# Lambda's powers prepared in the fourth instead of the third block of the first projection, with the background queue of the fourth block pumped from its step 15 on at a rate of 0.9

## The chip, the cores and the metric

The kernel runs on one core of a Trainium2 chip. The metric is the device time of one execution in microseconds (us). Before the change three runs gave 1845.58, 1846.15 and 1850.67 us; the median is 1846.15.

## What is computed

Two layers on a sequence of 256 frames of width 2048, in float32. Each layer modulates its input by a conditioning vector c, runs a token mixer of inner width 4096, and closes with a gated residual and a LayerNorm. The first mixer is gated linear attention (GLA), the second a complex diagonal state-space layer (S5).

```python
mod = jnp.einsum('bd,lde->lbe', jax.nn.silu(c), ada_w) + ada_b[:, None, :]
for i in range(DEPTH):
    shift, scale, gate = jnp.split(mod[i], 3, axis=-1)
    u = x * (1.0 + scale[:, None, :]) + shift[:, None, :]
    h = gla_mixer(u, ...) if i % N_MIXERS == 0 else s5_mixer(u, ...)
    x = layer_norm(DEEPNORM_ALPHA * x + (1.0 + gate[:, None, :]) * h, ln_g[i], ln_b[i])
```

In the GLA mixer `proj = u @ w_in` gives q, k, v, z and a low-rank gate. In the S5 mixer each of 256 groups of 16 channels has 64 complex states. Their eigenvalues lambda come from small tables, and what the change touches is this:

```python
dt = jnp.exp(log_dt.astype(f32))[:, None]
mag = jnp.exp(a_re * dt)
lb_re = mag * jnp.cos(a_im * dt)
lb_im = mag * jnp.sin(a_im * dt)
```

The kernel needs the powers lambda^1 to lambda^8 and a coefficient that scales the S5 input matrix B.

## The kernel before

Everything is issued by one Python program for one core; a scheduler then fixes the order of instructions on each engine by the program's order and by its own estimate of when an instruction's inputs and buffers are ready. So an instruction can be issued somewhat ahead of its place in the program, but each engine's queue is fixed when the kernel is built.

Matrix products run in a split form: `wload` brings a weight tile of 128x1024 (512 KB, two 128-row groups by 512 columns) by a DMA of SyncE's queue, and `split` (lines 145, 146) makes a high part `hi` by a copy on ScalarE (ACT) and a low part `lo` by a subtraction on VectorE (DVE). Six weight tiles and three `hi` and three `lo` buffers rotate. One step consumes one weight tile. A step for v (`mv_step`) is 12 matmuls of 512 columns, one for q and k (`st_step`, called q below) is 24 of 256 columns.

The first projection computes q, k and v of the first layer. It is cut into four blocks along the contraction, `blocks = ((0, 2), (2, 2), (4, 4), (8, 8))` in units of 128, so that it can start before all of the modulation is known. Each later block adds to what the block before has left in `vtok` and `qk`. The first two blocks have 12 steps each, the third has 24 (16 for v, then 8 for q), the fourth has 48 (16 for q, then 32 for v). The steps are counted through all blocks as j, and within a block as i. While a block runs, the modulation for the next one is made: loads of `ada_w` (tiles `a`, 1 MB, 8 KB per partition), matmuls `psa` from them, the columns `mods`, transposes of x (`psx`) and the split of u. These are set to steps by a table (`put_ada`, `put_u`, list `along`) and may not be issued before that step. The last of them, the u of the fourth block, stand at steps j = 42 to 47.

One pool, `s8`, of twelve buffers of 8 KB per partition holds very different tiles: four for u, two for q and k (`qk`), two for x (`xrow`, until the third block's end), the modulation loads `a`, and all the tiles of the S5 preparation.

Work that nothing in the projection needs is put between the steps in three ways:
- `prep_lambda` (lines 500 to 596) is a generator. `next(lam, None)` runs it up to its next `yield`. It loads three tables, yields three times, computes dt and the magnitude by a polynomial in many small DVE instructions, two Sin on ACT, the powers by doubling (1, 2, 4 at a time, into `pwr`, with `pwt` for products), and ends with 64 small matmuls for `l8`. It takes 13 calls, and holds three buffers of 8 KB: `lamst`, `pwr` and `pwt`. Before, it gets a call in each step of the third block; what is left would run at that block's end.
- `bg` is the background queue. `pump(rate)` adds the rate to a counter and issues an item for each whole unit. Its first 26 items are the S5 preparation: loads, `prep_pow(0)` and `prep_pow(1)` (ACT copies `pd`, PE transposes `pspw`, ACT copies `lc`, a write of `rec`), `prep_b` (six DVE products `bb`, then four times transposes `psrb` and a copy `rowsb`, a write) and `prep_c` (`cc`, `psrc`, `rowsc`). `prep_pow` and `prep_b` need lambda's powers. Behind them come 108 items of the modulation of later stages. Before, the fourth block pumps from its first step at 0.62.
- `gla_gate` is a generator for the GLA gate. It gets a call in each step of the fourth block from i = 20 (`GATE_AT`) on and takes 17. It asks for the two 8 KB tiles `ea` and `la` with its third call. Its result multiplies k, and then `qs` is made from q (three DVE instructions, line 832). The attention matmuls `psst` start right behind the fourth block and need `qs`.

Then come the z projection with the attention output, the output projection, and the S5 layer. The S5 layer reads `rec` and `l8`. All later stages pump the same queue `bg`.

Of the kernel before, what the change touches and what calls it, by code (L numbers as in the profile page):

```python
# [33 lines left out]
def trunk(ctx, tc, x, c, ln_g, ln_b, ada_w, ada_b, gla_w_in, gla_gate_w2, gla_gate_b, gla_norm_g,  # L34
# [61 lines left out]
    def pump(rate=1.0):  # L96
        pace[0] += rate
        while pace[0] >= 1.0:
            pace[0] -= 1.0
            if bg:  # L100
                bg.pop(0)()
# [276 lines left out]
    def issue_to(n):  # L378
        while len(issued) < min(n, len(wants)):
            issued.append(wload(win, *wants[len(issued)]))  # L380
# [89 lines left out]
    def prep_small():  # L470
        dr = rp.tile([P, 2, 16], F32, tag="row", name="dr", bufs=2)
        dma(dr, s5_d[0].rearrange("(h g i) -> g h i", h=2, i=16))
        ps = psx("psd")
        for h in range(2):
            PE.transpose(ps[:16, h * P:(h + 1) * P], dr[:, h, :], ident)
        S.copy(dT, ps[:16, 0:256])
        zt = rp.tile([P, 448], F32, tag="row", name="zt", bufs=2)
        V.memset(zt, 0.0)
        for i in range(2):
            wdma(dk[:, i * 448:(i + 1) * 448].rearrange("(r p) c -> p r c", p=P), zt.unsqueeze(1).to_broadcast([P, 4, 448]))  # L480
# [195 lines left out]
    lam = prep_lambda()  # L676
# [5 lines left out]
    for part in range(2):  # L682
        for j in range(4):
            bg.extend(ada_dve(1, part, j))
    V_RATE, Z_RATE, OP_RATE = 0.62, 0.944, 0.755
    KEEP = (4, 6)
    GATE_AT = 20
    SCAN_RATE = 1.728
# [114 lines left out]
    for n, steps in enumerate(all_steps):  # L803
        for i, f_ in enumerate(steps):
            if n < 3:

                issue_to(j + 6)
            f_()
            with tc.issue_after(last_lo[0]), tc.issue_after(last_mm[0]):
                for g_ in along.get(j, ()):  # L810
                    g_()
            j += 1
            if n == 2:
                next(lam, None)
            elif n == 3:
                if i == 3:
                    prep_small()
                pump(V_RATE)
                if i >= GATE_AT:
                    next(gate, None)  # L820
        if n == 2:
            for _ in lam:
                pass

    for _ in gate:
        pass
# [83 lines left out]
    for g in range(8):  # L910
# [9 lines left out]
        for f in range(4):  # L920
            i = (g * 4 + f) % 8
# [271 lines left out]
    for g in range(8):  # L1193
        banks = [psm(f"su{g}{f}") for f in range(4)]
        for kp in range(8):
# [12 lines left out]
            n = max(0, int(b_pace[0]))  # L1208
# [67 lines left out]
    for g in range(8):  # L1276
# [9 lines left out]
        for f in range(4):  # L1286
            i = (g * 4 + f) % 8
# [43 lines left out]
    for g in range(8):  # L1331
# [14 lines left out]
        for f in range(4):  # L1346
            i = g * 4 + f
# [112 lines left out]
```

## Time and profile before

| | |
|---|---|
| median of three runs | 1846.15 us |
| the profiled execution | 1846.54 us, its span 1844.7 us |
| PE busy | 1795.5 us, 97% of the span |
| DVE busy | 1422.5 us, 77% |
| ACT busy | 897.4 us, 49% |
| third block, v part | 105.5 to 170.0 us |
| third block, q part | 170.0 to 203.3 us |
| fourth block, q part | 203.3 to 257.7 us |
| fourth block, v part | 257.7 to 362.8 us |

PE is TensorE's matmul, DVE is VectorE, ACT is ScalarE, SP is SyncE, whose queue issues the loads. Times inside the trace count from the span's start. An engine's busy time is the union of its instructions; in a list of groups each instruction counts fully, so where neighbours overlap, as they do by some 0.09 us on DVE and ACT, the groups add up to a little more. A wait is idle time of the engine just before an instruction, put down to the instruction whose end released it.

### The profile page before, as it was taken

How to read it: one execution, taken by the hardware profiler on the slowest of the kernel's cores; microseconds unless marked ns; L12 is line 12 of the kernel's file. 1: busy time of each engine (PE TensorE's matmuls, PEld its weight loads, DVE VectorE, ACT ScalarE, POOL GpSimd, SP SyncE). 2: the span in 40 equal slices, each digit the busy share in tenths (PEclk: the TensorE clock that was granted, in tenths of full speed). 3: DMA queues.
4: the chain of work that ended last, by engine and by line, in shares of the span. 5: the costliest groups of instructions: out<-in, count | busy, mean ns of one | idle time of the engine just before them, and what ended most of it. 6: DMA issues, size and time to landing. Idle time of an engine off the chain costs nothing.

```text
span 1844.7 us, 33886 instructions
## 1 busy us (share of the span) xinstructions
PE 1795.5 (97%) x13619; PEld 1588.5 (86%) x13619; DVE 1422.5 (77%) x1890; ACT 897.4 (49%) x1252; POOL 72.7 (4%) x78
## 2 busy tenths in 40 slices
PE   7999999999999999999999999999999999999997
PEld 5776897899999888899999999988888888888885
DVE  4877657879989888697899689888677775557556
ACT  5433557556556333654454454545544444444332
POOL 0000000000000000002223200000000000000000
PEclk9999999999999999999999999999999999999999
DMA  9996875889889998465654477899688886668653
GB/s 343 386 333 248 294 244 164 279 261 325 291 286 317 333 353 281 163 220 158 183 151 147 139 214 222 235 246 238 224 276 264 276 271 206 191 189 325 194 184 92
DMA packets 243798, 449.48 MB, mean 244 GB/s; under 512 B 19572, under 2 KB 48942, under 8 KB 242358
## 3 DMA queue, kind: packets, MB, share of 16 engines
q1 hardware_dynamic: 239320, 436.02, 73.9%
q0 software_dynamic: 3552, 10.24, 1.8%
q8 instruction: 107, 1.75, 0.4%
q10 hardware_dynamic: 768, 1.05, 0.2%
q14 instruction: 51, 0.42, 0.1%
HBM read 432.81 MB, written 14.42 MB: 242 GB/s over the span
## 4 chain that ended last, share of the span: by engine, by line
PE 86%; DVE 8%; DMA 3%; ACT 2%; issue 2%; SPq 0%; DVEq 0%; ACTq 0%
PE gl L192 13%; PE gl L193 7%; PE op L168 6%; PE op L167 6%; PE op L169 6%; PE z L182 3%; PE z L180 3%; PE z L181 3%; PE sz L180 3%; PE v L168 3%; PE v L169 3%; PE sz L181 3%; PE sz L182 3%; PE v L167 3%; PE su L180 2%; PE su L182 2%
## 5 line engine op out<-in xcount | busy, mean ns | idle before, releaser
L146 DVE TENSOR_TENSOR logl<-wgl,higl 128x1024 fp32r<-128x1024 f32 x128 | 156.5, 1224 | 115.3 <-ACT higl L145 113.7
L145 ACT CAST higl<-wgl 128x1024 fp32r<-128x1024 f32 x128 | 134.4, 1051 | 172.2 <-PE gl L192 167.9
L192 PE MATMUL gl<-yb,higl 128*128 128x512 f32 x512 | 179.6, 395 | 0.0
L192 PE MATMUL gl<-yp,higl 128*128 128x512 f32 x512 | 179.3, 395 | 0.1
L145 ACT CAST hio<-wo 128x1024 fp32r<-128x1024 f32 x95 | 100.2, 1055 | 155.3 <-PE op L169 127.3
L146 DVE TENSOR_TENSOR loo<-wo,hio 128x1024 fp32r<-128x1024 f32 x95 | 116.2, 1225 | 67.2 <-ACT hio L145 63.7
L315 DVE SCALAR_TENSOR_TENSOR acc<-wa,cs,acc 128x512 f32<-128x512 f32 x217 | 162.2, 748 | 4.8 <-DMA wa<-in_ada_w 2.1
L180 PE MATMUL su<-u1h,hisu 128*128 128x256 f32 x512 | 153.5, 301 | 1.9 <-DVE vv L1108 1.9
L180 PE MATMUL sz<-u1h,hisz 128*128 128x256 f32 x512 | 149.7, 292 | 1.2 <-ACT zs L1290 1.2
L180 PE MATMUL z<-u0h,hiz 128*128 128x256 f32 x512 | 148.7, 290 | 0.0
L182 PE MATMUL su<-u1h,losu 128*128 128x256 f32 x512 | 145.7, 286 | 0.4 <-DVE losu L146 0.4
L181 PE MATMUL su<-u1l,hisu 128*128 128x256 f32 x512 | 145.8, 285 | 0.0
L182 PE MATMUL z<-u0h,loz 128*128 128x256 f32 x512 | 144.9, 283 | 0.6 <-DVE loz L146 0.6
L182 PE MATMUL sz<-u1h,losz 128*128 128x256 f32 x512 | 144.9, 283 | 0.0
L181 PE MATMUL sz<-u1l,hisz 128*128 128x256 f32 x512 | 144.7, 283 | 0.0
L181 PE MATMUL z<-u0l,hiz 128*128 128x256 f32 x512 | 144.7, 283 | 0.0
L193 PE MATMUL gl<-yb,logl 128*128 128x256 f32 x512 | 143.4, 280 | 0.0
L193 PE MATMUL gl<-yp,logl 128*128 128x256 f32 x512 | 142.0, 280 | 0.0
L145 ACT CAST hisz<-wsz 128x1024 fp32r<-128x1024 f32 x64 | 66.9, 1051 | 107.2 <-PE sz L181 55.1
L192 PEld LDWEIGHTS gl<-yb,higl 128*128 128x128 f32 x512 | 96.0, 188 | 22.6
L192 PEld LDWEIGHTS gl<-yp,higl 128*128 128x128 f32 x512 | 95.8, 188 | 22.6 <-issue 0.6
L145 ACT CAST hisu<-wsu 128x1024 fp32r<-128x1024 f32 x64 | 66.7, 1050 | 95.1 <-PE su L181 70.6
(322 smaller groups left out, 5019.8 us busy)
## 6 DMA issues: line engine op xcount, KB each, us to landing
wgl<-in_s_w_glu SPq DMA_DIRECT2D x128, 512.0 KB, 4.7
wa<-in_ada_w SPq DMA_DIRECT2D x116, 512.0 KB, 5.1
wv<-in_gla_w_in SPq DMA_DIRECT2D x64, 512.0 KB, 6.1
wz<-in_gla_w_in SPq DMA_DIRECT2D x64, 512.0 KB, 5.2
wsu<-in_s_w_in SPq DMA_DIRECT2D x64, 512.0 KB, 3.7
wsz<-in_s_w_in SPq DMA_DIRECT2D x64, 512.0 KB, 4.3
wo<-in_s_w_out SPq DMA_DIRECT2D x64, 512.0 KB, 4.5
a<-in_ada_w SPq DMA_DIRECT2D x31, 1024.0 KB, 10.7
```

Of the source, the lines that this page charges most:

```text
L145: S.copy(hi, w)
L146: last_lo[0] = V.tensor_tensor(lo, w, hi.bitcast(F32), op=ALU.subtract).ins
L167: PE.matmul(banks[tt], lhsT=uh, rhs=hi[:, kk, :], start=(k == first), stop=False)
L168: PE.matmul(banks[tt], lhsT=uh, rhs=lo[:, kk, :], start=False, stop=False)
L169: last_mm[0] = PE.matmul(banks[tt], lhsT=ul, rhs=hi[:, kk, :], start=False, stop=(k == last)).ins
L180: PE.matmul(o, lhsT=wh, rhs=u.hi(k), start=(k == first), stop=False)
L181: PE.matmul(o, lhsT=wh, rhs=u.lo(k), start=False, stop=False)
L182: last_mm[0] = PE.matmul(o, lhsT=wl, rhs=u.hi(k), start=False, stop=(k == last)).ins
L192: PE.matmul(banks[f], lhsT=hi[:, kk, fs], rhs=u.both(k), start=(k == 0), stop=False)
L193: PE.matmul(banks[f][:, :T], lhsT=lo[:, kk, fs], rhs=u.hi(k), start=False, stop=(k == last))
L315: V.scalar_tensor_tensor(acc[0], w[:, kk, :], cs[:, k:k + 1], acc[0], op0=ALU.mult, op1=ALU.add)
```

## The change

The call of `next(lam, None)` goes from the third block (n == 2) to the first 15 steps of the fourth (n == 3), and what remained of it behind the third block goes. In those 15 steps the background queue isn't pumped; from step 15 on it is, at 0.9 items per step where it was 0.62 in all 48 steps. `gla_gate` and `prep_small` stay at their steps.

```diff
-    V_RATE, Z_RATE, OP_RATE = 0.62, 0.944, 0.755
+    V_RATE, Z_RATE, OP_RATE = 0.9, 0.944, 0.755
+    LAM_TO = 15
...
-            if n == 2:
-                next(lam, None)
-            elif n == 3:
+            if n == 3:
                 if i == 3:
                     prep_small()
-                pump(V_RATE)
+                if i < LAM_TO:
+                    next(lam, None)
+                else:
+                    pump(V_RATE)
                 if i >= GATE_AT:
                     next(gate, None)
-        if n == 2:
-            for _ in lam:
-                pass
```

## Rows read from the trace of the kernel before

**Rows 1.** The page: busy time, share of the span and instructions of each engine; and the shares of the chain that ended last, by engine.

```profile
PE 1795.5 (97%) x13619; PEld 1588.5 (86%) x13619; DVE 1422.5 (77%) x1890; ACT 897.4 (49%) x1252; POOL 72.7 (4%) x78
...
PE 86%; DVE 8%; DMA 3%; ACT 2%; issue 2%; SPq 0%; DVEq 0%; ACTq 0%
```

**Rows 2.** Busy time by stretch: start and end, length, then busy us and (instructions) of PE, PEld, DVE, ACT, POOL, the granted clock, the DMA share, GB/s. The stretches are the v and the q part of the third block, the q and the v part of the fourth.

```profile
105.50:170.00 64.50, 59.02 (x358) 40.35 (x357) 51.78 (x125) 19.72 (x27) 0.00 (x0) 1.00 0.75 262
170.00:203.30 33.30, 33.30 (x277) 28.34 (x275) 21.16 (x37) 11.99 (x16) 0.00 (x0) 1.00 0.92 331
203.30:257.70 54.40, 52.53 (x437) 51.62 (x436) 35.16 (x47) 34.96 (x40) 5.00 (x5) 1.00 0.83 269
257.70:362.80 105.10, 102.87 (x482) 82.49 (x480) 79.64 (x95) 62.09 (x67) 3.65 (x4) 1.00 0.70 217
```

**Rows 3.** What PE waited for from 105 to 204 us, the third block: total us, times, longest.

```profile
PE v L168 <- DVE lov L146: 3.8, 2, 1.9
PE v L167 <- ACT hiv L145: 1.6, 1, 1.6
```

**Rows 4.** The same from 204 to 363 us, the fourth block.

```profile
PE v L168 <- DVE lov L146: 1.8, 3, 0.7
PE pspw L610 <- ACT pd L603: 1.0, 1, 1.0
PE pspw L610 <- ACT lc L612: 0.8, 2, 0.4
PE psrb L624 <- DVE bb L652: 0.5, 1, 0.5
```

**Rows 5.** What SyncE's queue waited for before modulation loads (L254) from 105 to 205 us: the release of an older load by its matmuls, and the release of `lamst`.

```profile
SPq L254 <- PE psa L275: 29.4, 6, 9.3
SPq L254 <- DVE crci L510: 9.7, 1, 9.7
```

**Rows 6.** DVE's timeline in the third block's v part, from the first writing of `pwr`: start, length, instruction.

```profile
152.37 0.49 DVE L510 TENSOR_TENSOR pwr<-lamst 128x128 f32<-128x128 f32 x2
...
155.54 1.22 DVE L146 TENSOR_TENSOR lov<-wv,hiv 128x1024 fp32r<-128x1024 f32 x1
...
160.49 1.22 DVE L146 TENSOR_TENSOR lov<-wv,hiv 128x1024 fp32r<-128x1024 f32 x1
```

**Rows 7.** Busy time of the third block's v part again, DVE's part (and, in the first row, ACT's) of the instructions that touch `lamst` alone, and of those that touch `pwt` alone.

```profile
105.50:170.00 64.50, 11.27 (x47) 0.51 (x2) 1.00 0.75 262
105.50:170.00 64.50, 8.04 (x18) 1.00 0.75 262
```

**Rows 8.** DVE's timeline: the first of `prep_b(0)`'s six products.

```profile
224.14 1.22 DVE L647 TENSOR_TENSOR bb<-bin,crci 128x1024 f32<-128x1024 f32 x1
```

**Rows 9.** ACT's groups by line from 204 to 258 us, the fourth block's q part: busy us, mean ns of one, idle before them.

```profile
L612 ACT ACTIVATE lc<-pspw,kst 128x512 f32<-128x512 f32 x4 | 4.4, 1208 | 0.0
L625 ACT COPY rowsb<-psrb 128x512 f32<-128x512 f32 x4 | 4.3, 1086 | 0.0
L612 ACT ACTIVATE lc<-pspw 128x512 f32<-128x512 f32 x4 | 4.1, 1138 | 0.0
L603 ACT COPY pd<-pwr 128x1024 f32<-128x1024 f32 x4 | 4.0, 1045 | 0.0
...
L669 ACT COPY cc<-cin 128x1024 f32<-128x1024 f32 x1 | 1.1, 1081 | 0.0
```

**Rows 10.** PE's groups by line: the transposes of `prep_pow` and `prep_b` in the fourth block's q part, and the matmuls for `l8` in the third block's v part.

```profile
L610 PE MATMUL pspw<-ident,pd 128*128 128x128 f32 x32 | 4.5, 280 | 1.9 <-ACT pd L603 1.0 <-ACT lc L612 0.8
L624 PE MATMUL psrb<-ident,bb 128*128 128x128 f32 x16 | 2.5, 278 | 0.0
...
L591 PE MATMUL psl<-ident,pwr 128*32 128x32 f32 x64 | 1.0, 199 | 0.0
```

**Rows 11.** PE's timeline: two neighbouring matmuls of a v step in the third block, and two of a q step in the fourth.

```profile
129.04 0.39 PE L167 MATMUL v<-hiv,u0h 128*128 128x512 f32 x1
129.27 0.39 PE L168 MATMUL v<-lov,u0h 128*128 128x512 f32 x1
...
218.08 0.28 PE L180 MATMUL q<-u0h,hiq 128*128 128x256 f32 x1
218.20 0.28 PE L181 MATMUL q<-u0l,hiq 128*128 128x256 f32 x1
```

**Rows 12.** Busy time by stretch, columns as in rows 2: the middle of the fourth block's v part.

```profile
290.00:326.00 36.00, 33.77 (x152) 26.24 (x151) 33.47 (x44) 30.81 (x34) 2.23 (x2) 1.00 0.55 164
```

**Rows 13.** ACT's groups by line from 258 to 363 us, the fourth block's v part: Exp (L726) and Ln (L729) of the gate with their table loads.

```profile
L726 ACT ACT_TABLE_LOAD x2 | 2.6, 1283 | 0.0
L729 ACT ACT_TABLE_LOAD x2 | 2.6, 1283 | 0.0
L729 ACT ACTIVATE ea<-ea,ones 128x1024 f32<-128x1024 f32 x2 | 2.3, 1152 | 0.0
...
L726 ACT ACTIVATE ea<-ea 128x1024 f32<-128x1024 f32 x2 | 2.1, 1062 | 0.0
```

**Rows 14.** The instructions that touch `qs` up to 365 us: count, shortest, median and longest in ns, then the first and last start.

```profile
L846 PE MATMUL psst<-qs,qk x20: 272/352/430, 362.8 to 364.8; 128*64 128x256 f32 x8, 128*64 128x192 f32 x8, 128*64 128x128 f32 x4
L832 DVE TENSOR_TENSOR qs<-qk,ft x3: 1219/1751/2285, 333.3 to 343.2; 128x2048 f32<-128x2048 f32 x1, 128x1536 f32<-128x1536 f32 x1, 128x1024 f32<-128x1024 f32 x1
```

**Rows 15.** SyncE's queue in order of time: lambda's first load.

```profile
101.94 0.46 SPq L513 DMA_DIRECT2D lamst<-in_s_a_re  x1
```

## The prediction

> **What bounds the kernel now.** I read the page's busy shares and its chain first: PE is busy for 97% of the span and holds 86% of the chain that ended last [rows 1]. So an edit pays only where PE stands idle, and costs only where it makes PE idle. Next I cut the time around the change into four stretches (the third block's v part, its q part, the fourth block's q part, its v part) and compared PE busy with each length [rows 2]: PE is idle for 5.5, 0.0, 1.9 and 2.2 us. That is all there is to win here. The PE waits name it. In the third block two waits for a weight split (`lov`) come to 3.8 us, one for `hiv` to 1.6 us [rows 3]; in the fourth, three waits for `lov` come to 1.8 us, `prep_pow` (`pspw`) to 1.8 us, `bb` to 0.5 us [rows 4]. No wait there is for a modulation load, though SyncE's queue stood 29.4 and 9.7 us before such loads for a buffer to come free [rows 5].
>
> **The change, part by part.** PE's work is the same; it is moved. So the sum is one of PE waits, against the profiled execution's own 1846.54 us (span 1844.7, so 1.8 us lie around it); the median of the runs is 0.4 us lower.
>
> *Third block.* The two `lov` waits are lambda's: in the DVE timeline a string of small instructions on `lamst`, `pwr` and `pwt` stands before the split that starts at 155.54 and, with evictions of v, before that at 160.49, the two for which PE waited [rows 6]. Without them DVE loses about 20 us of work: 11.3 us on `lamst`, 8.0 us on `pwt`, and some small ones [rows 7], so 51.8 of 64.5 us becomes about 32. Nothing is late next: ACT is busy for 19.7 us there [rows 2]. Term: -3.8 us (between -3.8 and -2, if some other DVE work is late in a wait's place). The 1.6 us wait for `hiv` at the block's start stays; lambda's arithmetic has not begun there. Three buffers come free for the modulation loads, and SyncE's queue loses lambda's three loads in this block; as PE waited for no such load, and was busy for all 33.3 us of the q part, I cost this at nothing. What hides it is the six weight tiles fetched ahead.
>
> *Fourth block, q part (16 steps).* Leaves: the background queue. `prep_b(0)`'s six products of 1.22 us go from DVE [rows 8]; from ACT go two `prep_pow`, 12.5 us (4.4 + 4.1 + 4.0), four `rowsb` copies, 4.3 us, and `cc`, 2.2 us [rows 9]. Comes: lambda, 13 pieces at steps 0 to 12; the first three only load and wait, so DVE's part falls into steps 3 to 12. DVE: 35.2 - 7.3 + 20 = about 48 us. PE: 52.5 busy, less 4.5 (`pspw`) and 2.5 (`psrb`), plus 1.0 for lambda's 64 small matmuls [rows 10], about 46.5 us. So DVE has more to do than PE in this part, where before it had less. A q step is 24 matmuls started 0.12 us apart [rows 11], 2.9 us, so ten steps are 29 us; DVE needs 10 splits at 1.14 (starts of neighbours, 1.22 each with overlap), 10 x 0.35 of `qk` and 20 for lambda, 35 us. It is 6 us short. The cushion: three split buffers let a split come up to two steps (5.8 us) after its buffer is released, less 1.05 for ACT's half and 1.22 for its own, 3.5 us. Left over: 2.5 us; I take +3, since lambda's last three pieces are dense (its `pwt` part) and the cushion is not full when they come. Bounds: 0, if the queue's order starts lambda earlier in DVE's idle time (the first product of `prep_b(0)`, of step 8, began at 224.1 us, some 7 steps of 2.9 us behind the part's start [rows 8], so a little ahead of its place), and 6, with no cushion at all.
>
> Behind a DVE instruction that is late stands the next split, and behind that PE: there is no other path. The l8 matmuls and the Sin pair move along; the loads pass SyncE's weights, which are not late. What lambda feeds beyond this block is `rec` and `l8`, and the S5 layer reads them first, so its lateness costs nothing there.
>
> *`prep_pow`.* Its 1.8 us of PE waits came because ACT's copies and PE's transposes depend on each other in turn, with ACT also splitting. It goes to steps 17 and 18 of the fourth block, in the v part. Same dependence, same price: 0 in the sum (-1.8 if hidden, +1.8 if doubled, as a v step is shorter).
>
> *Fourth block, v part (32 steps).* 29 items of the background queue were issued before (48 x 0.62), 29 are now (33 x 0.9): what comes after the block starts with the same queue. But 26 of them, the S5 preparation, now fall into steps 16 to 43, with `gla_gate` in steps 20 to 36. DVE: 79.6 + 7.3 = 87 of now some 110 us, 79%; ACT: 62.1 + 12.5 + 4.3 + 2.2 = 81, 74% [rows 2, 8, 9]. These are means; in the dense stretch from 290 to 326 us DVE is already at 33.5 of 36 us and ACT at 30.8, and there lie the 2.3 us of waits [rows 12]. By steps: a v step is 12 matmuls 0.23 apart [rows 11], 2.7 us. In steps 26 to 31 ACT has six splits (6), the gate's four table loads (5.1), its Exp and Ln (4.4), `cc0` and four `rowsc` copies (6.2) [rows 13]: 21.7 against 16.3 of steps and 0.5 of transposes and up: 3 to 5 us short. In steps 32 to 36 DVE has 5 x 1.75 for split and eviction, `prep_b(1)`'s 6.9, and 4.6 of the gate: 20.2 against 14.5, 5.7 short. Each is met by a cushion of 5.4 - 1.05 - 1.22 = 3.2 us: about 0.6 and 2.5 us of waits, 3.1 in all where 2.3 were. Term: +0.8. Bounds: -2.3 (all hidden) and +6.5 (no cushion, 8.8 less 2.3).
>
> A rule of the Trainium skill can be held against this. Perfetto Trace Analysis, section Identifying the Most-Contended Engine, says that for the vector and scalar engines the occupancy tells how contended they are. By it the v part, at 79% and 74%, would take the moved work for nothing, and the sum would be -0.8, 1845.7, too near to tell apart. Here the row of 290 to 326 us differs: the mean of the part before is 76% for DVE, and PE waited for it all the same.
>
> *The end of the block.* `gla_gate` keeps its steps, but shares ACT and DVE with more, and its two buffers (`ea`, `la`) are asked for while `prep_pow`'s tiles wait for their writes. The last `qs` starts at 343.2 us and lasts 1.2, and PE needs it at 362.8 [rows 14]: 18 us of cover. Lateness up to that costs nothing, beyond it one for one. Term: 0.
>
> Sum: -3.8 + 3 + 0 + 0.8 = 0.0. So 1846.5 for a profiled execution, 1846.1 on the scale of the median; I say 1846.
>
> **Rivals.** *A, faster: the moved work finds room.* Lambda's instructions spread over the q part, since 19 us of ACT work and 7 of DVE's leave it, and `prep_pow` hides behind longer gate steps: -3.8 - 1.8, 1841, or 1840 if some v waits go as well. For it: DVE is free for 19 us of the q part now. Against: the 48 us of DVE beside 46.5 of PE. Chance 0.15. *B, slower: the v part becomes bound by ACT and DVE.* Place: steps 17 to 36. Price: -3.8 + 4 in the q part, +6.5 in the v part, +0.9 of `prep_pow`: +7.6, 1854. It decides when the two shortages come one after the other without a rest, so that the second meets an empty cushion. For it: waits at 93% DVE before. Against: the gate and `prep_b(1)` overlap there already, and cost only 2.3. Chance 0.18. *C, the change does less than it says:* the scheduler moves lambda back into the third block, as it issues ahead of the program's order; then waits stay, 1846 to 1847. Against: lambda's first load went out at 101.9 us [rows 15], 4 us before the third block began, so the scheduler runs ahead by little more than a step. Chance 0.05. *D, the gate slips beyond its cover of 18 us:* +3 to +10; chance 0.03. My forecast has 0.59.
>
> **How the numbers follow.** About 0.3%, 5.5 us, is what a measurement of this kernel can tell from no change. Faster by more: most of A, 0.13. Slower: B and D, and a tail of the forecast, 0.19. Within: 0.68. The likeliest case alone spans -4 to +4, 1842 to 1850; the range reaches to A and B: 1840 to 1853.
>
> **What would show it.** PE waits for `lov` in the third block's v part gone: first term right. New waits of PE for `loq` in the fourth block's q part, some 3 us, with lambda on DVE just before them: second term right; none, then A. `pspw` waits of about 2 us, now between v steps. Waits for `lov` in the v part of 3 us, and ACT close to full in the middle of it; over 8 us, then B. A PE wait before `psst` would be D. If `lamst` is still written before the fourth block starts, C. The forecast is wrong if the time is outside 1842 to 1850.

## The result, and the profile after

The changed kernel takes 1853.43 us (median of 20 runs, 1849.06 to 1858.68) against 1847.96 us (20 runs, 1841.95 to 1852.02) for the kernel before, run beside it. The two medians are 5.5 us apart; the ratio over all these runs, which is used from here on, is 1.0036, with a 95% interval of 1.0028 to 1.0044. So it is slower by some 6.6 us, where the prediction said no change. The ratios of the experiments below are also each against runs of the kernel before, made beside them.

The page of the changed kernel gives the busy shares, as in [rows 1]:

```profile
PE 1797.3 (97%) x13619; PEld 1589.2 (86%) x13619; DVE 1422.1 (77%) x1890; ACT 897.8 (49%) x1252; POOL 70.2 (4%) x78
```

The counts are those of before and the busy times differ by 1.8 us at most on PE, DVE and ACT: the work is the same. The loss is in PE's idle time and, by 1.8 us at most, in PE's pace.

Busy time by stretch, columns as in [rows 2]; the first begins at 105.5 us as there, each next one at the first `q` or `v` of a block's part, and the last ends at the first `psst`:

```profile
105.50:165.80 60.30, 57.28 (x296) 39.84 (x295) 32.61 (x40) 18.41 (x20) 0.00 (x0) 1.00 0.95 338
165.80:198.60 32.80, 32.80 (x274) 27.98 (x273) 20.84 (x37) 11.80 (x16) 0.00 (x0) 1.00 0.60 194
198.60:249.60 51.00, 48.37 (x455) 47.37 (x454) 46.82 (x126) 20.91 (x30) 1.72 (x2) 1.00 0.72 224
249.60:367.20 117.60, 110.67 (x532) 89.06 (x530) 84.73 (x98) 76.64 (x82) 6.94 (x6) 0.99 0.71 223
```

Each of the first three is shorter than before (60.3, 32.8 and 51.0 where 64.5, 33.3 and 54.4 were), 8.1 us together. The fourth block's v part is 12.5 us longer: it has 7.8 us more of PE busy (50 PE instructions more, nearly all of them transposes that moved there, and the slow pace shown below) and 4.7 us more of PE idle. The granted clock of this stretch is 0.99.

The PE waits that replace those of [rows 3] (105 to 204 us):

```profile
PE v L167 <- ACT hiv L145: 1.6, 1, 1.6
PE v L168 <- DVE lov L146: 1.5, 1, 1.5
```

and those that replace [rows 4], up to 376 us, so that `psst` is in the window:

```profile
PE v L168 <- DVE lov L146: 4.8, 3, 3.6
PE psst L845 <- ACT sts L849: 2.0, 1, 2.0
PE q L182 <- DVE loq L146: 1.5, 1, 1.5
PE q L180 <- DVE qk L415: 1.1, 1, 1.1
PE pspw L610 <- ACT lc L612: 1.1, 2, 0.7
PE pspw L610 <- ACT pd L603: 0.9, 1, 0.9
```

The third block gave back 2.3 us of waits (5.4 to 3.1); from there on they grew from 4.1 to 11.4. Three of these waits were then followed to what stood ahead.

*The 1.5 us left in the third block.* DVE's timeline there (start, length, instruction, and in brackets the idle time before it and what ended it):

```profile
155.53 0.69 DVE L401 TENSOR_TENSOR vbig<-vbig,v 128x512 f32<-128x512 f32 x1 [2.48 <-PE v L169]
156.66 0.69 DVE L401 TENSOR_TENSOR vbig<-vbig,v 128x512 f32<-128x512 f32 x1 [0.44 <-PE v L169]
157.26 2.35 DVE L146 TENSOR_TENSOR lov<-wv,hiv 128x1024 fp32r<-128x1024 f32 x2
```

DVE stood idle for 2.48 us, not short of work: its next instruction in the queue was an eviction, which waits for PE's last matmul of that column group, and the split that PE needs next was queued behind it. ACT had made the high parts of both splits by 155.0:

```profile
153.94 1.06 ACT L145 CAST hiv<-wv 128x1024 fp32r<-128x1024 f32 x1 [1.66 <-PE v L169]
```

*The 3.6 us in the v part.* DVE's timeline up to the split that PE waited for:

```profile
315.85 1.22 DVE L146 TENSOR_TENSOR lov<-wv,hiv 128x1024 fp32r<-128x1024 f32 x1
316.98 1.28 DVE L401 TENSOR_TENSOR vbig<-vbig,v 128x512 f32<-128x512 f32 x2
318.18 1.22 DVE L647 TENSOR_TENSOR bb<-bin,crci 128x1024 f32<-128x1024 f32 x1
319.32 1.22 DVE L648 TENSOR_TENSOR bt<-bin,crci 128x1024 f32<-128x1024 f32 x1
320.45 1.22 DVE L650 TENSOR_TENSOR bb<-bin,crci 128x1024 f32<-128x1024 f32 x1
321.59 1.22 DVE L649 TENSOR_TENSOR bb<-bb,bt 128x1024 f32<-128x1024 f32 x1
322.72 1.22 DVE L146 TENSOR_TENSOR lov<-wv,hiv 128x1024 fp32r<-128x1024 f32 x1
```

Two evictions and four products of `prep_b(1)` stand in one row between two splits that start 6.9 us apart, where a v step is 2.7 us. What followed that wait is seen in the windows around it (columns as in [rows 2]):

```profile
318.00:321.00 3.00, 2.37 (x11) 1.62 (x9) 3.00 (x4) 1.48 (x2) 1.02 (x1) 1.00 0.89 259
321.00:324.00 3.00, 0.01 (x1) 0.01 (x1) 3.00 (x4) 0.00 (x0) 0.00 (x0) 0.94 0.90 265
324.00:327.50 3.50, 3.50 (x9) 2.82 (x10) 3.50 (x6) 0.00 (x0) 0.00 (x0) 0.56 0.52 150
327.50:331.00 3.50, 3.50 (x19) 2.94 (x18) 2.83 (x4) 3.00 (x5) 0.00 (x0) 1.00 0.59 164
```

Behind the wait the granted clock is 0.56, so most of that window at the lower of the two levels, 1.2 instead of 2.4 GHz, and only 9 PE instructions lie in it, where 19 (4 of them short transposes) lie in the next window of the same length. The 12 matmuls behind the wait start within 4.28 us (the first at 323.99, the instruction behind the last at 328.27); at the 0.23 us of [rows 11] they take 2.76. That is 1.5 us more, and it shows as busy time, in no wait.

*The 2.0 us before `psst`.* ACT's timeline at the block's end:

```profile
361.84 1.06 ACT L145 CAST hiz<-wz 128x1024 fp32r<-128x1024 f32 x1 [1.66 <-PE v L169]
370.44 1.99 ACT L145 CAST hiz<-wz 128x1024 fp32r<-128x1024 f32 x2 [7.54 <-DMA wz<-in_gla_w_in]
372.34 0.47 ACT L847 COPY sts<-psst 64x384 f32<-64x384 f32 x1
```

The copy of `psst` out of PSUM, for which PE waits, stands in ACT's queue behind two `hiz` copies of the z projection, and these wait 7.54 us for a weight load. In the kernel before the same copies waited for their load too, but only till 362.69:

```profile
362.69 1.99 ACT L145 CAST hiz<-wz 128x1024 fp32r<-128x1024 f32 x2 [4.15 <-DMA wz<-in_gla_w_in]
```

There `psst` began at 362.8 [rows 14], so the queue was free in time.

Up to the first matmul of the z projection this adds up: the third block's waits -2.3, the later waits +7.3, the slow step +1.5, together +6.5. Counted from the third block's start to the z projection's, the profile before has 262.95 us and the one after 269.47, so +6.5 as well. The two spans differ by 4.6 only (1844.7 and 1849.3): from the z projection's start to the end the profiles of all the kernels told of here lay between 1471.8 and 1476.5 us, in no order with their edits, so a single span is a blunt measure of these edits. I use the length to the z projection's start beside the timed ratio.

### The profile page after: what moved, and what is told of

The parts are those of the page before. It is cut to its first block, busy times and chain, and to the rows that moved or that the text cites. A ratio compares the mean times of both kernels' runs of the same rounds, so it can differ in the third digit from the quotient of the medians.

```text
span 1849.3 us, 33886 instructions
## 1 busy us (share of the span) xinstructions
PE 1797.3 (97%) x13619; PEld 1589.2 (86%) x13619; DVE 1422.1 (77%) x1890; ACT 897.8 (49%) x1252; POOL 70.2 (4%) x78
## 4 chain that ended last, share of the span: by engine, by line
PE 77%; DVE 10%; DMA 6%; ACT 3%; issue 3%; SPq 0%; DVEq 0%; ACTq 0%
PE gl L192 13%; PE gl L193 6%; PE op L167 6%; PE op L168 6%; PE op L169 6%; PE z L182 3%; PE z L180 3%; PE z L181 3%; PE sz L180 2%; PE v L168 2%; PE v L169 2%; PE v L167 2%; PE sz L182 2%; PE sz L181 2%; PE su L180 2%
```

## The experiments

The change does two things: it moves lambda, and it squeezes the background queue of the fourth block from 48 steps into 33. My theory after seeing the result (theory 1 of the expectations) was that the squeezing makes the loss and lambda's place is worth about nothing. Against it stood that lambda beside the q steps is what costs, and that the three freed buffers bring modulation loads forward that collide with others.

**Squeeze the queue alone.** On the kernel before; lambda stays in the third block.

```diff
-    V_RATE, Z_RATE, OP_RATE = 0.62, 0.944, 0.755
+    V_RATE, Z_RATE, OP_RATE = 0.9, 0.944, 0.755
...
-                pump(V_RATE)
+                if i >= 15:
+                    pump(V_RATE)
```

> Lambda stays in the third block as before; only the background queue of the fourth block starts at its step 15 and runs at 0.9. Theory 1 (density: the loss of the changed kernel is made in the fourth block's v part, where 26 preparation items are squeezed into steps 16 to 43): the v part's waits for lov rise from 1.8 to 4 to 6 us, PE waits some 2 us before psst, the third block keeps its 3.8 us, and the q part has no waits; ratio to before 1.003 to 1.005, so at least as slow as the change. Theory 2 (lambda's own arithmetic in the q part, with all that it delays, makes the loss): ratio 0.999 to 1.001.

Measured 1.0036 [1.0024, 1.0049], the whole of the loss. The waits of 204 to 376 us:

```profile
PE v L168 <- DVE lov L146: 4.8, 3, 3.6
PE psst L847 <- ACT sts L851: 2.0, 1, 2.0
PE pspw L610 <- ACT lc L612: 1.1, 2, 0.6
PE pspw L610 <- ACT pd L603: 0.9, 1, 0.9
```

The 3.6 and the 2.0 us are those of the changed kernel. What is missing is `loq` and `qk`: these 2.6 us are lambda's. So the loss belongs to the queue.

**Lambda in the fourth block beside a queue at the old rate.** On the changed kernel, `prep_c` first in the queue, since it doesn't need lambda:

```diff
-    bg.extend(lb0 + [lambda: prep_pow(0), lambda: prep_pow(1)] + lc0 + cb0 + lb1 + cc0 + lc1 + cb1 + cc1)
+    bg.extend(lc0 + cc0 + lc1 + cc1 + lb0 + [lambda: prep_pow(0), lambda: prep_pow(1)] + cb0 + lb1 + cb1)
...
-    V_RATE, Z_RATE, OP_RATE = 0.9, 0.944, 0.755
+    V_RATE, Z_RATE, OP_RATE = 0.62, 0.944, 0.755
...
-                else:
-                    pump(V_RATE)
+                pump(V_RATE)
```

> Lambda in the fourth block as in the change, but the background queue runs beside it from step 0 at the old rate 0.62, with prep_c for both halves first (it does not need lambda's powers). Theory 1: the v part's waits return to some 2 us, no wait before psst, the q part keeps some 2.6 us, the third block's gain of 2.4 us stays; ratio 0.998 to 1.001. Theory 2: the q part's waits are larger than 2.6 us and the ratio stays at 1.003 or above.

Measured 1.0056 [1.0043, 1.0069], worse than either theory allows. Its waits:

```profile
PE psrb L624 <- DVE bb L652: 5.2, 2, 4.2
PE psrb L624 <- ACT rowsb L625: 3.2, 1, 3.2
PE q L182 <- DVE loq L146: 2.5, 1, 2.5
```

PE now stops at its own transposes of `prep_b`. The longest of these waits in PE's timeline:

```profile
339.76 1.30 PE L624 MATMUL psrb<-ident,bb 128*128 128x128 f32 x5 [4.20 <-DVE bb L652]
```

All three lie in the v part (the others end at 306.8 and 311.5 us), long behind lambda's last instruction on DVE at 244.5 us: DVE makes the products between evictions, the gate and splits, and PE has the transposes ahead of the next v matmuls. Only the `loq` wait, at 240.5 us, is in the part where lambda runs. Nor are the waits all: from 105 us on they are 6.1 us more than in the kernel before, and the length to the z projection is 13.3 us more. The rest is pace, as the granted clock is 0.94 in both parts of the fourth block (199.3 to 255.4 and 255.4 to 376.9 us), where it was 1.00. The `psst` wait is gone. So a low mean rate isn't what protects; the place of single pieces seems to decide, but this run also changes the queue's order, so it does not tell which.

**Half the squeeze.** On the kernel before, the queue from step 8 on at 0.74.

```diff
-    V_RATE, Z_RATE, OP_RATE = 0.62, 0.944, 0.755
+    V_RATE, Z_RATE, OP_RATE = 0.74, 0.944, 0.755
...
-                pump(V_RATE)
+                if i >= 8:
+                    pump(V_RATE)
```

> Lambda stays in the third block, the background queue of the fourth block is issued from its step 8 on at 0.74 items per step (40 x 0.74 = 29.6, as many as 48 x 0.62 or 33 x 0.9). Theory 1, the closer the preparation of the S5 layer stands, the more of its ACT and DVE work collides with the splits: halfway between the two rates, so between 1.001 and 1.003, with v-part waits between 3 and 6 us. Rival, a matter of which pieces meet the gate and the Z loads by chance and not of the rate: no order between rate and time, so either 1.000 or 1.004.

Measured 1.0049 [1.0031, 1.0066]: no less than the full squeeze (the intervals overlap), and above the 1.001 to 1.003 of theory 1, which falls in this form. Two lines of its waits, and DVE's timeline ahead of the longest of them:

```profile
PE v L168 <- DVE lov L146: 5.6, 4, 3.6
...
PE psst L847 <- ACT sts L851: 0.8, 1, 0.8
```

```profile
316.81 1.22 DVE L648 TENSOR_TENSOR bt<-bin,crci 128x1024 f32<-128x1024 f32 x1
317.94 0.69 DVE L401 TENSOR_TENSOR vbig<-vbig,v 128x512 f32<-128x512 f32 x1
318.54 1.22 DVE L649 TENSOR_TENSOR bb<-bb,bt 128x1024 f32<-128x1024 f32 x1
319.68 0.68 DVE L401 TENSOR_TENSOR vbig<-vbig,v 128x512 f32<-128x512 f32 x1
320.27 1.22 DVE L651 TENSOR_TENSOR bt<-bin,crci 128x1024 f32<-128x1024 f32 x1
321.41 1.22 DVE L146 TENSOR_TENSOR lov<-wv,hiv 128x1024 fp32r<-128x1024 f32 x1
```

Again products of `prep_b(1)` and two evictions between a v step's splits. In the kernel before, the first of these six products started at 290.6 us and the last at 307.0, with other instructions between most of them. In both profiles the longest wait comes from a cluster, of products that come as late as the evictions of a column group. Half the squeeze was not cheaper than the whole.

**Hold the freed buffers.** On the changed kernel; three 8 KB tiles are kept through the third block and do nothing.

```diff
+            held = [s8t(f"held{i}", [8]) for i in range(3)]
+            for h_ in held:
+                V.memset(h_, 0.0)
...
+            if n == 2 and i == 22:
+                hs = cp.tile([P, 8], F32, name="hs")
+                for h_ in held:
+                    V.tensor_copy(hs, h_)
```

> The changed kernel with three buffers of 8 KB kept occupied through the third block (three small memsets at its start, three small copies at its step 22), so that the modulation loads have as few buffers as before. My theory (the freed buffers are worth nothing to PE): the third block's waits and the time are those of the changed kernel, ratio 1.0025 to 1.0045. Rival (the loads need them): new PE waits before psa or in the third block of 2 us or more, ratio above 1.005.

Measured 1.0031 [1.0017, 1.0046], the time of the changed kernel, with the same PE waits to 0.1 us, though SyncE's queue stood 10.4 us for one of the held buffers. The length to the z projection is 272.2 us, 2.7 more at the same waits: this profile has more time at the lower clock, in the q part (0.68 from 242 to 247 us, 1.00 in the changed kernel) and behind the 3.6 us wait (0.66 from 324 to 334 us, 0.83 from 321 to 331 us in the changed kernel). The buffers are worth nothing for PE here, neither gain nor loss.

Three edits, each on one of the three waits, then told whether a wait's length comes back when its cause goes.

**The eviction behind the next split.** On the changed kernel; for the third and the fourth block the two evictions of a column group are issued after the next weight's split.

```diff
+            while pend:
+                pend.pop(0)()
...
+                        if k0:
+                            with tc.issue_after(last_lo[0]):
+                                V.tensor_tensor(o, o, banks[cg][tt], op=ALU.add)
...
+                if k0 >= 4 and cg < 7:
+                    pend.append(evict)
```

> The changed kernel, but in the third and fourth block an eviction of v (vbig) is issued behind the next step's weight split instead of ahead of it. Theory: the 1.5 us wait for lov left in the third block comes from a split that stands behind two evictions which themselves wait for PE; it goes, and part of the v part's waits with it: 1.5 to 3 us less than the changed kernel, ratio 1.002 to 1.003. Rival (the split is late for another reason, its hi half or its load): no difference from the changed kernel, 1.0028 to 1.0044.

Measured 1.0018 [1.0007, 1.0028]. The third block's 1.5 us wait is gone, and its v part is 58.1 us where 59.8 were: the order on DVE had caused it. The 3.6 us wait stays, since there the products are what stands ahead. In this profile no slow step followed it, so some 1.5 of the 3.0 us by which its length is shorter are the clock's:

```profile
321.00:324.00 3.00, 0.95 (x4) 0.82 (x5) 3.00 (x3) 0.00 (x0) 0.00 (x0) 1.00 0.55 162
324.00:327.50 3.50, 3.50 (x19) 2.89 (x18) 3.50 (x7) 1.85 (x3) 0.00 (x0) 1.00 0.48 150
```

On the kernel before, the same edit:

> The kernel before with one edit alone, v's eviction in the third and fourth block behind the next split. In the changed kernel this took 0.0018 off. Theory 1, it relieves the split that stands behind evictions where DVE is crowded: before is less crowded in the fourth block but has lambda in the third, so 0.999 to 1.000, the third block's two waits for lov stay at 3 to 4 us. Rival, the eviction delays the split everywhere: 0.998 or below, with the third block's lov waits gone.

Measured 0.9998 [0.9987, 1.0010]. The third block's two `lov` waits went from 3.8 to 2.5 us, which neither expectation had, and the fourth block's three from 1.8 to 2.4. The third block's v part is no shorter for it (64.6 us, 64.5 before), since the granted clock was 0.75 from 155 to 160 us, where it was 1.00.

**The products in pairs.** On the changed kernel; `prep_b`'s six products become three items of the queue with two each, and the rate goes to 1.02, so that as much is issued.

```diff
-        return [load], [comp] + to_rows(lambda: got["b"], lambda s, i: s[:, :, i], t, 256, f"b{t}")
+        return [load], [comp, two, two] + to_rows(lambda: got["b"], lambda s, i: s[:, :, i], t, 256, f"b{t}")
...
-    V_RATE, Z_RATE, OP_RATE = 0.9, 0.944, 0.755
+    V_RATE, Z_RATE, OP_RATE = 1.02, 0.944, 0.755
```

> The changed kernel with the six products of prep_b as three queue items of two instead of one item of six, the queue's rate raised to 1.02 so that the same work is issued in the block. Theory (the longest wait of the v part, 3.6 us, comes from four products that stand ahead of a split on DVE, and the half-clock window of 3.4 us that follows it adds some 1.7): that wait falls below 1.5 us and no half-clock window lies in the v part; 3 to 5 us less than the changed kernel, ratio 1.0005 to 1.002. Rival (DVE is simply full there, so the wait only moves): the waits for lov in the v part stay at 4 to 5 us in total, ratio 1.003 to 1.004.

Measured 1.0030 [1.0015, 1.0045]. Its v wait:

```profile
PE v L168 <- DVE lov L146: 4.0, 4, 1.5
```

The longest wait falls from 3.6 to 1.5 us, but the sum only from 4.8 to 4.0, and the time is not told from the changed kernel's: that is what the rival said. In the profile the v part is 2.1 us shorter, and no slow step lies in it (1.5 us by the count above, not the 1.7 of the expectation); but the q parts are 1.8 us longer, as the granted clock is 0.66 from 242 to 247 us, behind the `loq` wait that the changed kernel has too, and the z projection is 1.1 us longer. The Trainium skill, Perfetto Trace Analysis, section Optimizing Scalar/DVE Operations, advises to break up instructions where such an engine isn't saturated yet causes idle time on others. DVE was busy for 72% of the v part (84.73 of 117.6 us), and splitting up the group of six instructions (none of them was broken up itself) did shorten the longest wait, but here that alone paid nothing that the runs can tell.

**The `psst` copies first.** On the changed kernel; the second to fourth splits of the z projection are ordered behind the last copy of `psst`.

```diff
+            with tc.issue_after(last_sts) if g == 0 and 1 <= kp < 4 else nullcontext():
+                w = split(wload(win, 2 * kp, 6144 + g * 512, f"z{g}{kp}"), f"z{g}{kp}")
```

> The changed kernel, with the hi copies of the z projection's second to fourth weight tile ordered behind the last copy of sts on ACT. Theory (the 2.0 us before psst are ACT's queue: a hi copy that waits for its weight load stands ahead of the sts copies): the wait before psst goes, z starts some 2 us earlier after the first psst, and the ratio is 1.002 to 1.003, unless the first z steps wait for their split instead. Rival (the sts copies are late by themselves, or the load is what everything waits for): the wait turns into one of the same length before z, ratio unchanged at 1.0028 to 1.0044.

Measured 1.0030 [1.0017, 1.0044]. The 2.0 us wait is gone and `psst` to z takes 6.0 us, as before the change (8.2 after); the v waits are unchanged. So ACT's order was the cause of that wait; its 2 us, 0.1%, are at the edge of what these runs tell.

**All three edits** on the changed kernel:

> The changed kernel with three edits together: evictions of v behind the next split, prep_b in three items of two, the z splits behind the sts copies. If the three waits are separate causes: -1.5, -3 to -5 and -2 us, which leaves the kernel 0 to 2 us ahead of the one before, ratio 0.998 to 1.0005. If lambda in the fourth block costs by itself, the ratio stays above 1.001.

Measured 1.0008 [0.9998, 1.0018]: the loss is gone but for 1.5 us that the interval can't tell from none. That lies between the two cases of the expectation. The length to the z projection is 263.4 us, where 269.5 and, before the change, 262.9 were.

**The same with lambda back in the third block,** and the squeezed queue kept:

> The three relieving edits together (v's eviction behind the next split, the products of prep_b in pairs, the sts copies ahead of the copies for z), with the dense queue from step 15, but lambda back in the third block. Against the kernel with these edits and lambda in the fourth (1.0008), this is lambda's place alone. Theory 1: lambda's place is worth nothing, 0.999 to 1.002. Rival: with the v part relieved, the third block's waits that lambda's move removed show, 2 us: above 1.002; or the fourth q part's waits for loq show, 2.6 us: below 0.999.

Measured 1.0017 [1.0008, 1.0025], length 265.6. Its third block has the waits

```profile
PE v L168 <- DVE lov L146: 2.5, 2, 1.9
PE v L167 <- ACT hiv L145: 1.6, 1, 1.6
```

that lambda's move takes away in part. So lambda's place in the fourth block is better by 2.1 us in the profiles here, and by 1.2 (270.7 against 269.5) in the unrelieved pair. In both pairs the kernel with lambda in the third block had a stretch at the lower clock there, worth some 1.5 us, and its partner had none (last section); without it 0.6 us and nothing are left. The intervals of the ratios overlap, so in time lambda's place is not told from nothing.

**Two of the edits on the kernel before,** the eviction behind the split and the products in pairs (at a rate of 0.705):

> The kernel before with the two edits that apply to it: evictions of v behind the next split and prep_b in three items of two at a rate of 0.705. If the order on DVE is what makes PE wait, the v part's 2.3 us fall below 1.5 and the third block's 3.8 us (lambda) stay: ratio 0.998 to 1.000. If not, 1.000 to 1.002.

Measured 1.0005 [0.9994, 1.0016], length 262.9, as without them. The theory's condition failed: the v part's waits are 3.0 us and not below 1.5, and the third block's 3.8 fell to 2.5. No version beat the kernel before.

The lengths in one view (us, from the profiles; from the first matmul of the third block's v part, of its q part, of the fourth block's v part and of `psst`, each to the next, the last to the z projection's first):

| kernel | third v | both q parts | fourth v | psst | sum | timed ratio |
|---|---|---|---|---|---|---|
| before | 64.5 | 87.3 | 105.2 | 6.0 | 262.9 | 1 |
| the change | 59.8 | 83.8 | 117.6 | 8.2 | 269.5 | 1.0036 |
| squeeze alone | 65.5 | 79.2 | 117.6 | 8.3 | 270.7 | 1.0036 |
| half squeeze | 66.0 | 84.4 | 112.1 | 7.0 | 269.6 | 1.0049 |
| lambda, old rate | 59.8 | 88.9 | 121.5 | 6.0 | 276.3 | 1.0056 |
| buffers held | 59.9 | 85.3 | 118.7 | 8.2 | 272.2 | 1.0031 |
| eviction late | 58.1 | 83.9 | 116.1 | 8.4 | 266.5 | 1.0018 |
| products in pairs | 59.8 | 85.6 | 115.5 | 7.9 | 268.9 | 1.0030 |
| copies first | 59.8 | 83.9 | 117.5 | 6.0 | 267.2 | 1.0030 |
| all three edits | 58.1 | 83.8 | 115.5 | 6.0 | 263.4 | 1.0008 |
| the same, lambda back | 64.7 | 79.4 | 115.5 | 6.0 | 265.6 | 1.0017 |
| before, eviction late | 64.6 | 87.3 | 105.4 | 6.0 | 263.4 | 0.9998 |
| before, two edits | 64.7 | 86.3 | 105.9 | 6.0 | 262.9 | 1.0005 |

The third v part is about 60 us or less whenever lambda is out of it. The last two columns put the kernels in nearly the same order, but for the held buffers, whose profile has more time at the lower clock than that of the changed kernel; that is why I trust the lengths.

## Why the prediction was wrong

The time lies 0.4 us above the range, and the forecast of no change had 0.68. On the prediction's own scale the ratio gives 1852.8 (1.0036 times 1846.15), just inside the range; what failed is the sum, by 6.5 us. By its own terms, in us:

| step | predicted | measured | miss |
|---|---|---|---|
| third block's waits | -3.8 | -2.3 | +1.5 |
| fourth block, q part | +3 | +2.6 | -0.4 |
| `prep_pow` | 0 | +0.2 | +0.2 |
| fourth block, v part: waits | +0.8 | +2.5 | +1.7 |
| fourth block, v part: pace | none | +1.5 | +1.5 |
| end of the block | 0 | +2.0 | +2.0 |
| sum | 0.0 | +6.5 | +6.5 |

*Third block: mechanism right, size off.* "Nothing is late next" was wrong. I looked at how busy the other engines are, and ACT was free; but what took the wait's place was an idle DVE, held by an eviction at the head of its queue. The lower bound that I gave, -2, was for such a case. Moving the eviction removed the wait.

*Fourth block's q part: right.* The forecast was new `loq` waits of some 3 us with lambda just before them; 1.5 on `loq` and 1.1 on `qk` came, and both are absent where lambda stays in the third block. The `qk` wait is for an eviction, and not by the next split, which the prediction called the only path. DVE's 48 us of work were 46.8.

*`prep_pow`: right*, 2.0 us of waits where 1.8 were. *The freed buffers: right*, worth nothing.

*The v part: the term mis-sized.* The place was named (steps 32 to 36, `prep_b(1)` beside evictions and the gate) and the shortage there too, 5.7 us. The error was the cushion of 3.2 us that I set against it: I took it as full, for work spread evenly over the steps. In the trace six such instructions stood in one row, and the wait was 3.6 us where I had 2.5 for this place; with the others it came to 4.8 in place of 3.1. This is rival B in kind, and its condition, shortages that meet an empty cushion, was the right one to ask about; of its price of +6.5 for this part, +2.5 came as waits and +1.5 as pace. That B's total of +7.6 lies near the measured +6.5 is in part luck, as 2.0 of this came from the end of the block, which B has not. The means of 79% and 74% (measured 72% for DVE, 65% for ACT) were no help in telling.

*The pace behind a wait: not in the prediction at all.* Every wait was costed at its own length.

*The end of the block: the wrong path.* I watched the gate (rival D). Its sign, a PE wait before `psst`, came, but from another cause. The last `qs` began at 353.4 us (343.2 before) and lasted 1.2, so it was done 12.6 us ahead of `psst`: the gate slipped by 10 us and its cover held. What came late was a weight load for z, and through ACT's fixed order it held the copies that PE needed. That `hiz` waited 4.15 us for a load at 362.7 could have been read in the trace of before; I had listed what each edit delays on ACT and DVE, but not what an end of the block 4.4 us later and with more writes in flight would meet there. Why that load was later is not settled: the last write of the S5 preparation was issued at 358.3 us where it was 348.4 before, which fits, but no run moved it alone. In the ten profiles with ACT's order left as it was, this write was issued 6 to 9 us ahead of the first `psst` in the six that have the wait, and 12 to 14 us ahead in the four that have none.

What stays open: which of the queue's pieces must not meet, as a rule. The half squeeze was no cheaper, so the rate alone doesn't tell; what the scheduler would have to avoid is not shown.

## What to carry to other kernels

When background work is moved or squeezed, read the new order on each in-order queue at the places where the critical consumer is fed: several long instructions in one row, or one that waits for something else, ahead of what PE needs are the price, and the mean share of the engine doesn't show them. Separate a change's two parts in the first experiment; here the part that the change is named for was worth about nothing, and the squeeze of the queue that came along with it made the loss. Where one wait is removed, ask what stands at the head of the idle engine's queue, not whether the engine has time.

## What the runs showed of the hardware that was not expected

A wait can cost more than its length. Behind the 3.6 us wait the granted clock was 0.56 of full speed in a window of 3.5 us, and 12 matmuls took 4.28 us in place of 2.76. The same wait of about 3.6 us was followed by such a stretch in five profiles (the changed kernel, both squeezes, the held buffers, the copies first), but not in that with the late eviction. The waits of up to 1.9 us that the third block has with lambda in it were followed by none in the kernel before:

```profile
154.00:158.00 4.00, 2.11 (x10) 1.43 (x9) 3.93 (x14) 1.05 (x1) 0.00 (x0) 1.00 0.29 68
158.00:162.00 4.00, 2.06 (x10) 1.41 (x9) 3.94 (x8) 1.05 (x1) 0.00 (x0) 1.00 1.03 375
162.00:166.00 4.00, 4.00 (x53) 2.68 (x53) 3.94 (x6) 0.00 (x0) 0.00 (x0) 1.00 0.21 81
```

and by one in each of the five other kernels with lambda in the third block, as here where only the queue was squeezed, though the third block's program is the same:

```profile
155.00:160.00 5.00, 3.11 (x13) 2.17 (x12) 4.80 (x16) 1.05 (x1) 0.00 (x0) 0.91 0.44 143
160.00:164.00 4.00, 2.60 (x7) 1.60 (x6) 3.23 (x7) 1.04 (x1) 0.00 (x0) 0.69 0.95 342
164.00:168.00 4.00, 4.00 (x53) 2.71 (x53) 3.93 (x7) 0.00 (x0) 0.00 (x0) 1.00 0.03 8
```

The Trainium skill, Perfetto Trace Analysis, section Matmul Optimizations, says that the matmul engine scales its power by utilization and so should be given back-to-back batches. These rows agree in that the lower clock came behind idle time; that the same idle time brought it in one profile and not in the next is not in that rule. With the waits of the kernel before (3.8 and 1.6 us), the half squeeze's third v part is 1.5 us longer (66.0 against 64.5), so there too such a stretch cost about 1.5 us. The profile of the kernel before, without it, is the exception among the six.

The 1.5 us behind the 3.6 us wait are what one execution shows. For all of them there is an estimate, as each run has its mean granted clock on record: 0.9925 in 23 runs of the kernel before (beside the first experiments), 0.9915 in the 20 of the changed kernel, 0.9888 in the 6 with lambda at the old rate. A difference of 0.001 over some 1850 us is 1.9 us of full speed. So some 2 of the 6.6 us are the clock's, and some 7 of the 10 us of lambda at the old rate.
